# A decoder layer in split float32: weight blocks split in two pieces instead of four, and the pass with the rest of the weights put last

## The chip, the cores and the metric

The kernel runs on one core of a Trainium2 chip. The metric is the device time of one execution, in microseconds (us). An execution uses these engines: TensorE (PE, with its weight loads shown apart as PEld), VectorE (DVE), ScalarE (ACT), GpSimd (POOL), and the DMA queue that SyncE (SP) issues.

## The reference, cut to what matters

One layer of a hybrid decoder on 512 tokens of width 1024, all in float32. An RMS norm; one wide product with w_in, whose columns feed a gated short convolution, a gated delta rule with 8 heads (queries, keys, values, z, and two small gates), and two merge gates; the two branches' output products, merged and projected by w_o; a residual; a second norm; a convolutional FFN of inner width 2816; a final norm.

```python
h = rmsnorm(x, norm_mix_g[l])
proj = h @ w_in[l]
bg, cg, xv, q, k, v, z, a, b, ga, gb = jnp.split(proj, pts, axis=-1)
y_a = short_conv_branch(bg, cg, xv, conv_a_w[l]) @ w_a_out[l]
y_b = gdn_branch(q, k, v, z, a, b, ...) @ w_b_out[l]
mix = jax.nn.sigmoid(ga) * y_a + jax.nn.sigmoid(gb) * y_b
x = x + mix @ w_o[l]
h = rmsnorm(x, norm_ffn_g[l])
x = x + conv_ffn(h, w_up[l], ffn_conv_w[l], w_down[l])
return rmsnorm(x, norm_final_g)
```

## The kernel before

**Three products for one.** Each float32 matrix is split into a rounded part and the rest: w = wh + wl for the weights, x = xh + xl for the activations. A product w x is then three TensorE products, wh xl + wl xh + wh xh, added up in one PSUM bank. The type of the parts is float32r.

**Blocks and jobs.** The weights come in blocks of 1 MB: 8 slices of 128 rows by 256 columns (`col_job`), or 2 slices of 128 rows by all 1024 columns (`row_jobs`, for w_o and w_down). A block is loaded into `raw` by one DMA (L131) and split by `Block.split` (L133 to L146): ACT casts a piece into wh (L143), DVE subtracts it from raw and writes wl (L144). A piece has 512 columns, so a block takes four pieces. raw, wh and wl have two buffers each. `run_jobs` (L148) walks over all blocks in turn: at the head of a job it finishes the split of the job's block, hands the next block's split to the queue `splits`, loads the block after that, and emits the job's products.

**Products.** A column job makes two tiles of 128 output columns by 512 tokens, each in its own PSUM bank, by `products` and `mm3` (L112): with 8 row slices that is 24 products a tile, 48 a block. `mm3` first goes over the 8 slices with a product wh xl and a product wl xh each, and then over the 8 slices with wh xh. A row job has the tokens on the partitions; for each token tile and half of the columns, `part` (L918) makes, for each of its two slices, xl wh, xh wl and xh wh in turn (the activations are the stationary operand there).

**What sets the order.** Every matrix product goes through `mm` (L103). After every fourth product of 512 columns it calls `tick`, which advances the waiting pieces of other work by one step each: the delta rule's scan (`backs`), its triangular inverse (`mids`), its front part (`chains`), two evacuations (`evacs`), and last one piece of the next block's split (`splits`). From this order of emission the framework makes each engine's queue; an engine works its queue in order.

**The start.** x comes as four tiles of 128 tokens. ACT squares and sums a tile (L315), DVE turns the sum into a mean (L320), POOL raises it to the power -1/2 (L321), DVE scales the tile (L326), PE transposes it (L331), and ACT and DVE write the transposed input in its two parts (L341, L343), tiles 0 and 1 as the first half of the tokens, tiles 2 and 3 as the second. The first products (16 gate columns, and the first key block `k_block`) run on the first half while the second is made. For this part the order of DVE, ACT and POOL is that of the program text, written out by hand (L347 on). Around the change it reads:

```python
ks = Task(k_block.split())
norm_x(2)
ks.step()
scale_x(2)
norm_x(3)
ks.step()
scale_x(3)
ks.finish()
```

**The delta rule's stage.** From about 25 to 325 us the products of the four head pairs' queries, keys, values and z run, with the delta rule's small products between them: transposes (L484), the scan (L680 and L681 for the state's reads, whose result DVE completes as r in L683; L693 with r, completed by DVE as vn in L695; L702 and L713 with vn). Then come the short convolution, the merge and w_o, the FFN's first product (two column blocks at a time), and its second.

Of the kernel before, what the change touches and what calls it, by code (L numbers as in the profile page):

```python
# [9 lines left out]
F32 = mybir.dt.float32  # L10
F32R = mybir.dt.float32r
AF = mybir.ActivationFunctionType
ALU = mybir.AluOpType
# [20 lines left out]
class Task:  # L34
    """A stretch of emission that is resumed piece by piece between slabs of matrix products."""

# [21 lines left out]
def layer_kernel(ctx, tc, x, norm_mix_g, w_in, conv_a_w, gdn_conv_w, gdn_A_log, gdn_dt_bias,  # L58
# [20 lines left out]

# [1 line left out]
    chains, mids, backs, evacs, splits = deque(), deque(), deque(), deque(), deque()  # L81
# [17 lines left out]
    def drain(queue):  # L99
        while queue:  # L100
            advance(queue, 1)

    def mm(o, a, b, start, stop):  # L103
        pe.matmul(o, lhsT=a, rhs=b, start=start, stop=stop)  # L104
        nmm[0] += o.shape[-1]
        if nmm[0] >= SLAB * S:
            nmm[0] -= SLAB * S
            tick()
# [3 lines left out]
    def mm3(o, pairs, order=KO):  # L112
        n = len(pairs)
        pairs = [pairs[k] for k in order]
        for i, (ah, al, bh, bl) in enumerate(pairs):
            mm(o, ah, bl, i == 0, False)
            mm(o, al, bh, False, False)
        for i, (ah, al, bh, bl) in enumerate(pairs):
            mm(o, ah, bh, False, i == n - 1)

# [1 line left out]
    class Block:  # L122
# [10 lines left out]
        def split(self):  # L133
            a, b = self.a, self.b
            if self.wh is not None:
                return
            self.wh = wp.tile([P, a, b], F32R, tag="wh", name=nm("wh"))
            self.wl = wp.tile([P, a, b], F32R, tag="wl", name=nm("wl"))
            h = max(1, 512 // b)
            for a0 in range(0, a, h):  # L140
                for b0 in range(0, b, 512):
                    sl = (slice(None), slice(a0, min(a, a0 + h)), slice(b0, min(b, b0 + 512)))
                    act.copy(out=self.wh[sl], in_=self.raw[sl])  # L143
                    dve.tensor_tensor(out=self.wl[sl], in0=self.raw[sl], in1=self.wh[sl].bitcast(F32),  # L144
                                      op=ALU.subtract)
                    yield  # L146

    def run_jobs(jobs):  # L148
        jobs[1][0].load()
        for i, (block, use) in enumerate(jobs):  # L150
            Task(block.split()).finish()
            drain(splits)
            if i + 1 < len(jobs):
                splits.append(Task(jobs[i + 1][0].split()))
            if i + 2 < len(jobs):
                jobs[i + 2][0].load()
            use(block.wh, block.wl)
# [33 lines left out]

# [1 line left out]
    ident = const.tile([P, P], F32, name="ident")  # L193
# [12 lines left out]

# [1 line left out]
    p2 = ExitStack()  # L208
# [6 lines left out]
    tbd = [dram.tile([4, 8, 32, 32], F32, name=f"tbd{p}") for p in range(4)]  # L215
# [1 line left out]
    ab_block = Block(lambda: cols(w_in[0], C_AB, 16), ND, 16)  # L217
    k_block = Block(lambda: cols(w_in[0], C_K, GW), ND, GW)
    HS = S // 2

    # both parts of the 16 columns side by side: two passes give four products
    def ab_products(o, lo, hi):
# [18 lines left out]
    def constants():  # L241
        pool.memset(triu, 1.0)
        pool.affine_select(out=triu, in_=triu, compare_op=ALU.is_ge, fill=0.0, base=0,
                           pattern=[[1, P]], channel_multiplier=-1)
        pool.memset(ones, 1.0)
        # mask16[j, i]: within a block of 32, j in its first half and i in its second
        pool.memset(full, 0.0)
        pool.memset(full.rearrange("p (b t c) -> p b t c", t=2, c=16)[:, :, 1, :], 1.0)
        f3 = full.rearrange("p (b t) -> p b t", t=32)
        pool.affine_select(out=f3, in_=f3, compare_op=ALU.is_ge, fill=0.0, base=0,  # L250
                           pattern=[[-32, 4], [0, 32]], channel_multiplier=1)
        pool.affine_select(out=f3, in_=f3, compare_op=ALU.is_ge, fill=0.0, base=15,
                           pattern=[[32, 4], [0, 32]], channel_multiplier=-1)
        for q in range(4):
            pool.tensor_copy(out=mask16[32 * q:32 * q + 32, :], in_=full[32 * q:32 * q + 32, 32 * q:32 * q + 32])
        # blocks of 16, one to a partition: -1 below the diagonal
        pool.memset(nlow, -1.0)
        pool.affine_select(out=nlow, in_=nlow, compare_op=ALU.is_gt, fill=0.0, base=0,
                           pattern=[[1, 16], [-1, 16]], channel_multiplier=0)
        pool.memset(TTf, 0.0)  # L260
        pool.memset(T64, 0.0)
        for p in range(4):
            nc.sync.dma_start(out=tbd[p].rearrange("q f r c -> (q f r c)").rearrange("(p n) -> p n", p=64),
                              in_=T64.rearrange("p f c -> p (f c)"))

    with tc.tile_pool(name="st1", bufs=1) as st1:
# [80 lines left out]
        with tc.manual_schedule(engines={mybir.EngineType.DVE, mybir.EngineType.Activation, mybir.EngineType.Pool}):  # L347
# [12 lines left out]
            ks = Task(k_block.split())  # L360
# [3 lines left out]
            norm_x(3)  # L364
            ks.step()
            scale_x(3)
# [120 lines left out]
    def front(pr, st):  # L487
# [54 lines left out]
        yield  # L542
        # values and queries by rows
        vs, ssq = tl("vs", 2), tl("ssq", 2, (P, 8))
# [13 lines left out]
        yield VREAD  # L558
        # inverse of the unit triangular factor: blocks of 16 by substitution, then doubled
        dve.tensor_tensor(out=TB, in0=UB.rearrange("p j i -> p i j"), in1=nlow, op=ALU.mult)  # L560
# [101 lines left out]
    def back(pr, st, kn, A, ap_, vs, ssq):  # L662
# [3 lines left out]
        junk = tl("junk", 1, (P, P))  # L666
        # scan over the chunks
        on = vs
# [146 lines left out]

# [1 line left out]
    p3 = ExitStack()  # L817
# [92 lines left out]

# [1 line left out]
    def row_jobs(w, nk, xs, finish, pre, early):  # L912
# [5 lines left out]
        def part(g, t):  # L918
            ts_ = slice(t * P, (t + 1) * P)
            x_ = xs()  # L920
            wh, wl = ws[g]
            for hf in range(2):
                hs = slice(hf * 512, (hf + 1) * 512)
                for kk in range(2):
                    k = 2 * g + kk
                    xh, xl = x_[0][:, k, ts_], x_[1][:, k, ts_]
                    mm(acc[t][hf], xl, wh[:, kk, hs], k == 0, False)
                    mm(acc[t][hf], xh, wl[:, kk, hs], False, False)
                    mm(acc[t][hf], xh, wh[:, kk, hs], False, k == nk - 1)

# [20 lines left out]

# [1 line left out]
    p7 = ExitStack()  # L953
# [49 lines left out]

# [1 line left out]
    gates = {}  # L1005
# [106 lines left out]
```

## Time and profile before

| what | value |
|---|---|
| median of 3 runs | 1000.38 us (999.54 to 1001.76) |
| span of the profiled execution, first to last instruction | 998.5 us |
| median of the runs less that span | 1.9 us |
| PE instructions | 5602 |
| DVE, ACT, POOL instructions | 1090, 931, 101 |
| HBM read and written | 93.27 MB and 3.42 MB, 97 GB/s over the span |
| granted TensorE clock, mean | 0.999 |

The profile lists the profiled execution by its span alone, so the table puts the median of the runs beside it. Busy time is the time in which an engine has at least one instruction under way. TensorE's products overlap, so the length shown for one (0.39 us for 512 columns) is more than the time by which it moves the queue on; that is the distance from one start to the next. A row of a group shows its line, engine, operation, operands and count, then the busy time and the mean length, then the idle time of the engine ahead of it and what ended most of that. A row of the list of waits shows who waited for whom, the total in us, how many times, and the longest. In a timeline a row shows start, length, the instruction and how many were merged into the row.

### The profile page before, as it was taken

To read this page: it belongs to the slowest core of one execution; us is meant where nothing else is said; L and a number is where in the kernel's file an instruction comes from. 1 tells how busy PE (TensorE), PEld (TensorE's weight loads), DVE (VectorE), ACT (ScalarE), POOL (GpSimd) and SP (SyncE) were. 2 spreads that over 40 slices of the span, in tenths; PEclk is the share of its full clock that TensorE was granted. 3 is DMA by queue.
4 is the path that set the end of the run, shared out by engine and by line. 5 is a ranking of instruction groups with operands and counts; after the bars stand their busy time and mean duration, and the time that the engine had idled before them with its cause. 6 is when DMAs were issued, how large, how long until landed. Compare 5 with 4: busy or idle time off the path is not lost.

```text
span 998.5 us, 14009 instructions
## 1 busy us (share of the span) xinstructions
PE 986.6 (99%) x5602; PEld 822.5 (82%) x5602; DVE 545.8 (55%) x1090; ACT 426.2 (43%) x931; POOL 64.3 (6%) x101
## 2 busy tenths in 40 slices
PE   8999999999999999999999999999999999999997
PEld 5887888888888888888888888988888888888886
DVE  6777776897434434542253553675665666532235
ACT  6695666665353322322331232454444444421123
POOL 3331201202010000000000000000000000000000
PEclk9999999999999999999999999999999999999999
DMA  7343232232212232223223252332223223223212
GB/s 223 105 133 94 72 93 86 72 93 57 88 44 85 85 119 93 85 87 124 85 88 124 85 190 84 106 117 96 85 90 121 85 86 126 85 87 124 84 43 85
DMA packets 95409, 97.60 MB, mean 98 GB/s; under 512 B 20299, under 2 KB 88176, under 8 KB 95344
## 3 DMA queue, kind: packets, MB, share of 16 engines
q1 hardware_dynamic: 95344, 96.70, 30.3%
q8 instruction: 44, 0.72, 0.3%
q14 instruction: 21, 0.17, 0.1%
HBM read 93.27 MB, written 3.42 MB: 97 GB/s over the span
## 4 chain that ended last, share of the span: by engine, by line
PE 96%; DVE 1%; issue 1%; ACT 1%; DMA 0%; SPq 0%; POOL 0%; POOLq 0%; ACTq 0%
PE ps L104 88%; PE ps L484 1%; PE ps L519 1%; PE ps L713 1%; PE ps L693 1%; PE ps L702 1%; PE ps L681 1%; PE ps L680 1%; PE ps L656 0%; PE ps L650 0%; DMA raw<-in_w_in_dram 0%; PE ps L991 0%; ACT hT L341 0%; PE ps L603 0%; PE ps L594 0%
## 5 line engine op out<-in xcount | busy, mean ns | idle before, releaser
L104 PE MATMUL ps<-hT,wh 128*128 128x512 f32 (+1 forms) x1184 | 371.2, 391 | 0.3 <-ACT wh L143 0.3
L144 DVE TENSOR_TENSOR wl<-raw,wh 128x512 fp32r<-128x512 f32 x324 | 211.7, 692 | 160.5 <-ACT wh L143 160.1
L104 PEld LDWEIGHTS ps<-hT,wh 128*128 128x128 f32 x1184 | 218.0, 188 | 41.1 <-ACT wh L143 0.6
L143 ACT CAST wh<-raw 128x512 fp32r<-128x512 f32 x324 | 178.6, 618 | 170.5 <-PE ps L104 162.3
L104 PE MATMUL ps<-hT,wl 128*128 128x512 f32 (+1 forms) x592 | 227.0, 385 | 0.3 <-DVE wl L144 0.3
L104 PE MATMUL ps<-h,wh 128*128 128x512 f32 (+1 forms) x768 | 220.8, 372 | 0.0
L104 PEld LDWEIGHTS ps<-h,wh 128*128 128x128 f32 x768 | 140.1, 188 | 24.9
L104 PE MATMUL ps<-h,wl 128*128 128x512 f32 (+1 forms) x384 | 140.2, 371 | 0.0
L104 PEld LDWEIGHTS ps<-hT,wl 128*128 128x128 f32 x592 | 111.4, 188 | 20.5 <-DVE wl L144 0.5
L104 PE MATMUL ps<-wh,aT 128*128 128x512 f32 x352 | 108.5, 389 | 0.0
L104 PEld LDWEIGHTS ps<-h,wl 128*128 128x128 f32 x384 | 72.3, 188 | 12.5
L104 PEld LDWEIGHTS ps<-wh,aT 128*128 128x128 f32 x352 | 66.1, 188 | 13.7
L104 PE MATMUL ps<-wl,aT 128*128 128x512 f32 x176 | 68.5, 389 | 0.0
L188 DVE SCALAR_TENSOR_TENSOR cv<-ps,wA,cv 128x511 f32<-128x511 f32 (+2 forms) x72 | 53.5, 743 | 11.2 <-ACT cv L185 10.4
L188 DVE SCALAR_TENSOR_TENSOR g<-ps,wF,g 128x511 f32<-128x511 f32 (+1 forms) x44 | 32.9, 747 | 48.2 <-ACT g L185 47.9
L188 DVE SCALAR_TENSOR_TENSOR v<-ps,wF,v 128x511 f32<-128x511 f32 (+1 forms) x44 | 32.8, 747 | 34.6 <-ACT v L185 34.3
L104 PE MATMUL ps<-wh,mix 128*128 128x512 f32 x128 | 40.1, 391 | 0.0
L104 PE MATMUL ps<-ya,wh 128*128 128x512 f32 x128 | 39.6, 389 | 0.0
L104 PE MATMUL ps<-yb,wh 128*128 128x512 f32 x128 | 39.6, 389 | 0.0
L104 PEld LDWEIGHTS ps<-wl,aT 128*128 128x128 f32 x176 | 33.0, 188 | 6.9
L185 ACT ACTIVATE g<-ps,wF 128x512 f32<-128x512 f32 x22 | 15.2, 690 | 38.9 <-PE ps L104 38.9
L185 ACT ACTIVATE v<-ps,wF 128x512 f32<-128x512 f32 x22 | 15.2, 690 | 38.6 <-PE ps L104 38.6
(227 smaller groups left out, 970.0 us busy)
## 6 DMA issues: line engine op xcount, KB each, us to landing
raw<-in_w_in_dram SPq DMA_DIRECT2D x36, 1024.0 KB, 5.1
raw<-in_w_up_dram SPq DMA_DIRECT2D x22, 1024.0 KB, 5.1
raw<-in_w_down_dram SPq DMA_DIRECT2D x11, 1024.0 KB, 4.9
raw<-in_w_a_out_dram SPq DMA_DIRECT2D x4, 1024.0 KB, 5.7
raw<-in_w_b_out_dram SPq DMA_DIRECT2D x4, 1024.0 KB, 5.6
raw<-in_w_o_dram SPq DMA_DIRECT2D x4, 1024.0 KB, 6.7
Dm<-gtd SPq DMA_DIRECT2D x4, 512.0 KB, 3.9
x<-in_x_dram SPq DMA_DIRECT2D x4, 512.0 KB, 6.8
```

The source lines that it names most:

```text
L104: pe.matmul(o, lhsT=a, rhs=b, start=start, stop=stop)
L143: act.copy(out=self.wh[sl], in_=self.raw[sl])
L144: dve.tensor_tensor(out=self.wl[sl], in0=self.raw[sl], in1=self.wh[sl].bitcast(F32), op=ALU.subtract)
L185: act.activation(out=dst, in_=src, func=AF.Copy, scale=wcol(taps - 1))
L188: dve.scalar_tensor_tensor(out=dst[:, sh:], in0=src[:, :S - sh], scalar=wcol(j), in1=dst[:, sh:], op0=ALU.mult, op1=ALU.add)
L484: pe.transpose(out=o[:, n * P:(n + 1) * P], in_=src[:, n * P:(n + 1) * P], identity=ident)
L519: pe.matmul(o[:, i], lhsT=kqs[:, a, h, 0, sl], rhs=kqs[:, b, h, :, sl], start=a > 0, stop=a + b == 0)
L680: pe.matmul(o[:, 0:P], lhsT=kq[:, h, 0, sl], rhs=St[h], start=True, stop=True)
L681: pe.matmul(o[:, P:2 * P], lhsT=kq[:, h, 1, sl], rhs=St[h], start=True, stop=True)
L693: pe.matmul(o[:, 0:P], lhsT=TTf[:, f, :], rhs=rs[h], start=True, stop=True)
L702: pe.matmul(o2[:, 0:P], lhsT=kn[:, f, :], rhs=vns[h], start=True, stop=True)
L713: pe.matmul(o[:, 0:P], lhsT=A[:, f, :], rhs=vns[h], start=True, stop=True)
```

## The change

Four edits that belong to the two in the title; the rest of the diff takes out comments and moves nothing.

- `mm3`: three loops over the slices instead of two: wh xh, then wh xl, then wl xh. The pass with the rest of the weights comes last.
- `part` in the row jobs: for both slices xh wh and xl wh, then for both slices xh wl.
- `Block.split`: a step takes half of the block's slices with all their columns, 4 x 256 or 1 x 1024, which is 1024 columns. A block takes two steps instead of four. In the start one `ks.step()` is taken out, so the key block's two steps are the first `ks.step()` and `ks.finish()`.
- `run_jobs`: `drain(splits)` stands ahead of finishing the job's own split instead of behind it.

```diff
         for i, (ah, al, bh, bl) in enumerate(pairs):
-            mm(o, ah, bl, i == 0, False)
-            mm(o, al, bh, False, False)
+            mm(o, ah, bh, i == 0, False)
+        for ah, al, bh, bl in pairs:
+            mm(o, ah, bl, False, False)
         for i, (ah, al, bh, bl) in enumerate(pairs):
-            mm(o, ah, bh, False, i == n - 1)
+            mm(o, al, bh, False, i == n - 1)
...
-            h = max(1, 512 // b)
-            for a0 in range(0, a, h):
-                for b0 in range(0, b, 512):
-                    sl = (slice(None), slice(a0, min(a, a0 + h)), slice(b0, min(b, b0 + 512)))
-                    act.copy(out=self.wh[sl], in_=self.raw[sl])
-                    dve.tensor_tensor(out=self.wl[sl], in0=self.raw[sl], in1=self.wh[sl].bitcast(F32),
-                                      op=ALU.subtract)
-                    yield
+            for a0 in range(0, a, a // 2):
+                sl = (slice(None), slice(a0, a0 + a // 2))
+                act.copy(out=self.wh[sl], in_=self.raw[sl])
+                dve.tensor_tensor(out=self.wl[sl], in0=self.raw[sl], in1=self.wh[sl].bitcast(F32),
+                                  op=ALU.subtract)
+                yield
...
         for i, (block, use) in enumerate(jobs):
+            drain(splits)
             Task(block.split()).finish()
-            drain(splits)
...
             norm_x(3)
-            ks.step()
             scale_x(3)
             ks.finish()
...
-                for kk in range(2):
-                    k = 2 * g + kk
-                    xh, xl = x_[0][:, k, ts_], x_[1][:, k, ts_]
-                    mm(acc[t][hf], xl, wh[:, kk, hs], k == 0, False)
-                    mm(acc[t][hf], xh, wl[:, kk, hs], False, False)
-                    mm(acc[t][hf], xh, wh[:, kk, hs], False, k == nk - 1)
+                xs_ = [(kk, x_[0][:, 2 * g + kk, ts_], x_[1][:, 2 * g + kk, ts_]) for kk in range(2)]
+                for kk, xh, xl in xs_:
+                    mm(acc[t][hf], xh, wh[:, kk, hs], 2 * g + kk == 0, False)
+                    mm(acc[t][hf], xl, wh[:, kk, hs], False, False)
+                for kk, xh, xl in xs_:
+                    mm(acc[t][hf], xh, wl[:, kk, hs], False, 2 * g + kk == nk - 1)
```

## The prediction

> **What bounds the kernel now.** I read the profile page first, then the busy times by stretch, then the list of TensorE's (PE's) own waits, and last the timelines of the places that these point to.
>
> ```profile
> span 998.5 us, 14009 instructions
> PE 986.6 (99%) x5602; PEld 822.5 (82%) x5602; DVE 545.8 (55%) x1090; ACT 426.2 (43%) x931; POOL 64.3 (6%) x101
> ...
> 0.00:25.00 25.00, 20.29 (x119) 14.59 (x120) 16.51 (x40) 17.12 (x39) 8.95 (x27) 1.00 0.73 223
> 25.00:325.00 300.00, 299.26 (x2438) 251.69 (x2436) 206.28 (x540) 176.98 (x473) 50.65 (x66) 1.00 0.29 85
> 325.00:992.00 667.00, 667.00 (x3050) 556.22 (x3048) 320.90 (x507) 230.47 (x417) 4.12 (x7) 1.00 0.30 99
> 992.00:998.50 6.50, 0.02 (x1) 0.00 (x0) 2.12 (x6) 1.59 (x5) 0.54 (x1) 0.78 0.21 81
> ```
>
> The rows by stretch give its length, then the busy time of PE, weight load, DVE (VectorE), ACT (ScalarE) and POOL, then the granted clock. From 325 to 992 us PE has no idle time at all, from 25 to 325 us it lacks 0.74 us, in the first 25 us it lacks 4.7 us, and the last 6.5 us are the end after its last product. DVE and ACT are well below full in every stretch. So the kernel is a queue of matrix products, and time can come or go in three ways only: idle PE at the start, idle PE in the gated-delta-rule stage (25 to 325 us), or another pace of the products.
>
> ```profile
> PE ps L484 <- DVE vs L732: 0.7, 1, 0.7
> PE ps L331 <- DVE xr L326: 0.6, 1, 0.6
> PE ps L104 <- DVE wl L144: 0.3, 1, 0.3
> PE ps L104 <- ACT wh L143: 0.3, 1, 0.3
> ```
>
> These are PE's waits, apart from two before 8 us. The split of the weights (wh on L143, the rest wl on L144) holds PE up twice, 0.3 us each, both in the first block. Nowhere later does PE wait for weights.
>
> The pace of the products is read from two timelines, one of the FFN's first product and one of its second (start, length, instructions merged into the line):
>
> ```profile
> 755.89 0.39 PE L104 MATMUL ps<-h,wl 128*128 128x512 f32 x1
> 756.12 2.20 PE L104 MATMUL ps<-h,wh 128*128 128x512 f32 x9
> 758.16 0.39 PE L104 MATMUL ps<-h,wl 128*128 128x512 f32 x1
> ...
> 905.04 0.39 PE L104 MATMUL ps<-wl,aT 128*128 128x512 f32 x1
> 905.27 0.61 PE L104 MATMUL ps<-wh,aT 128*128 128x512 f32 x2
> 905.72 0.39 PE L104 MATMUL ps<-wl,aT 128*128 128x512 f32 x1
> ```
>
> A run of nine wh products advances by (758.16 - 756.12) / 9 = 0.227 us each. A wl product followed by a wh product advances by 0.23. In the second FFN product three take 0.68 us, again 0.227 each. Runs and alternation cost the same.
>
> **The change, part by part.** *Order of the passes.* The number of products, their shapes and their count per PSUM bank stay as they are. At 0.227 us in a run and in alternation the new order costs nothing, as long as pace depends only on shape. It also keeps the place of the other engines' work: that is handed out after every fourth product, whichever pass it belongs to. What moves is which half of a block is needed when. wl is wanted 16 products (3.6 us) into each tile instead of at its first product, and wh is released eight products (1.8 us) before the end of a block instead of at the end, wl the other way round. PE never waits for either after the start, so I cost this at nothing. The cover is the whole block: 48 products of 0.227 us are 10.9 us, in which two new pieces, one behind the other on two engines, take about 3.5. Were the cover gone, each block would wait a first cast and a first subtract, about 2.3 us.
>
> *Swap of the two statements at the head of a job.* Where a split has been started, both orders finish it before the products; where it hasn't, both emit all of it there. Nothing changes.
>
> *Pieces of 1024 columns.* 324 casts and 324 subtracts become 162 of each. The rows for the price of a piece:
>
> ```profile
> L144 DVE TENSOR_TENSOR wl<-raw,wh 128x512 fp32r<-128x512 f32 x324 | 211.7, 692 | 160.5 <-ACT wh L143 160.1
> L231 DVE TENSOR_TENSOR ab<-raw,ab 128x128 fp32r<-128x128 f32 x1 | 0.3, 286 | 0.0
> L143 ACT CAST wh<-raw 128x512 fp32r<-128x512 f32 x324 | 178.6, 618 | 170.5 <-PE ps L104 162.3
> L230 ACT CAST ab<-raw 128x128 fp32r<-128x128 f32 x1 | 0.3, 300 | 0.2 <-DMA raw<-in_w_in_dram 0.2
> ```
>
> DVE: (692 - 286) / 384 = 1.06 ns a column, so 692 + 512 x 1.06 = 1.23 us. ACT: (618 - 300) / 384 = 0.83 ns, so 618 + 424 = 1.04 us. Busy time falls to 162 x 1.23 = 199 us on DVE (from 211.7) and 162 x 1.04 = 169 us on ACT (from 178.6): some 12 and 10 us, on engines that don't set the end. After the start that is worth nothing.
>
> *The start.* Here a longer piece matters, because ACT, DVE and POOL work in an order written out by hand. It runs: norm of x tile 2, piece of k, scale of tile 2, norm of tile 3, piece of k, scale of tile 3, rest of k. The change takes the second "piece of k" out and makes the first one twice as long.
>
> ```profile
> 14.02 0.67 ACT L143 CAST wh<-raw 128x512 fp32r<-128x512 f32 x1
> ...
> 14.71 0.69 DVE L144 TENSOR_TENSOR wl<-raw,wh 128x512 fp32r<-128x512 f32 x1 [0.35 <-ACT wh L143]
> ...
> 14.73 0.38 PE L104 MATMUL ps<-hT,wh 128*128 128x256 f32 x1 [0.30 <-ACT wh L143]
> 15.32 0.75 DVE L326 TENSOR_SCALAR xr<-xt,rt 128x1024 f32<-128x1024 f32 x1
> ...
> 15.46 0.38 PE L104 MATMUL ps<-hT,wl 128*128 128x256 f32 x1 [0.35 <-DVE wl L144]
> ...
> 15.69 0.28 PE L104 MATMUL ps<-hT,wh 128*128 128x256 f32 x1
> ...
> 15.80 0.28 PE L104 MATMUL ps<-hT,wl 128*128 128x256 f32 x1
> 15.98 0.15 DVE L320 TENSOR_SCALAR rt<-sst 128x1 f32<-128x1 f32 x1
> 16.21 0.55 POOL L321 TENSOR_TENSOR rt<-rt,nhalf 128x1 f32<-128x1 f32 x1 [1.22 <-DVE rt L320]
> 16.22 0.41 PE L331 MATMUL ps<-ident,xr 128*128 128x128 f32 x2
> ...
> 16.88 0.75 DVE L326 TENSOR_SCALAR xr<-xt,rt 128x1024 f32<-128x1024 f32 x1
> ```
>
> Before: the cast ends at 14.69, the subtract runs from 14.71, the scale of tile 2 (L326) starts at 15.32 and ends at 16.07, and PE transposes from 16.22. Ahead of that PE has done four products of k (14.73 to 15.80). After: the cast runs 14.02 to 15.06, the subtract from 15.10 to 16.33. DVE starts an instruction some 0.08 us before the last one's end (15.32 against 14.71 + 0.69), so the scale starts at 16.25, ends at 17.00, and PE can transpose from 17.15. The longer piece holds half of the k slices instead of a quarter, and the new order needs only wh first, so PE again has four products of that tile to do (from 15.1 to 15.6) and then nothing that stands ahead of the transposes. At 17.15 it is where it was at 16.22: 0.93 us late.
>
> Does this heal later? Queued behind the longer subtract on DVE are that scale, then the mean of tile 3 (15.98 before, now 16.9), POOL's power behind it, then the scale of tile 3: 17.8 instead of 16.88. Those feed the second half of the transposed input, so it is late by the same amount and the distances stay. From 17.15 PE has work without a gap: eight transposes, then 12 products that need only wh (its second cast ends near 17.1), then the transposes of tile 3, then the wl pass. With PE full from there to 992 us nothing gives the time back.
>
> The bounds: a piece of 0.75 us, the DVE row for 1024 columns of another operation, would make it +0.45, and so would four products of the second k tile, if they come forward into the gap (4 x 0.12). Two old pieces behind each other, 2 x 0.69 = 1.38, would make it +1.08. I take 0.93, because the 512 and 128 column rows are the same operation. [...]
>
> *The sum.* 998.5 us of span + 0.93 = 999.4. The median of the three runs is 1000.38, 1.9 us above the profiled span, which I carry over: **1001.3 us**.
>
> **The rivals.** *Stalls in the delta-rule scan (slower).* Between 25 and 325 us DVE is 69% busy, and the scan goes PE, DVE, PE. A longer subtract in front of a scan step makes PE's queue wait. One such place, DVE's rows and then PE's next step:
>
> ```profile
> 297.93 1.29 DVE L144 TENSOR_TENSOR wl<-raw,wh 128x512 fp32r<-128x512 f32 x2
> 299.13 0.60 DVE L683 SCALAR_TENSOR_TENSOR r<-ps,neG,vs 128x128 f32<-128x128 f32 x2
> 299.65 0.68 DVE L144 TENSOR_TENSOR wl<-raw,wh 128x512 fp32r<-128x512 f32 x1
> 300.51 0.61 DVE L695 TENSOR_SCALAR vn<-ps,ap 128x128 f32<-128x128 f32 x2 [0.17 <-PE ps L693]
> ...
> 301.46 0.61 PE L702 MATMUL ps<-vn,kn 128*128 128x128 f32 x4
> ...
> L144 DVE TENSOR_TENSOR wl<-raw,wh 128x512 fp32r<-128x512 f32 x78 | 53.5, 711 | 10.9 <-ACT wh L143 10.7
> ```
>
> With 1.23 us the piece at 299.65 would end at 300.88, and vn would start at 300.80 instead of 300.51: 0.29 late, against 301.46 - 301.12 = 0.34 us of slack before PE's step. That speaks against, and so does the row at 297.93: two old pieces back to back already take 1.29 us ahead of a scan step. For it speaks that 0.05 us is thin and that one wait of 0.7 us on DVE stands there today. The stage holds 78 / 2 = 39 new pieces; if eight cost the full 0.29, that is 2.3 us on top of the start: 1003.6. It decides from four such pieces on (four are 1.2 us, which takes the sum over 1002.4). [...]
>
> *The gap closes instead (faster).* The first wl wait (0.35) goes because wl comes last, the start's loss is filled by other products, and less DVE time lets the 0.74 us wait in the delta-rule stage go: 1000.38 - 0.35 - 0.74 = 999.3. The wait at L484 follows a POOL operation rather than a split, which speaks against. [...] If the start's loss alone is filled, the time stays at 1000.4.
>
> *The order changes the pace.* The new order puts products with the same moving operand, or the same kind of stationary one, behind each other in ways that the trace doesn't show. One ns on each of the 3050 TensorE instructions between 325 and 992 us is 3.05 us: 1004.4, or 998.2 the other way. The equal 0.227 us in run and alternation speaks against both.
>
> **How the numbers follow.** Forecast 1001.3 (own range 1000.6 to 1002.2): 0.56. Scan stalls, 1003.6: 0.18. Gap closed or nothing moved, 999.3 to 1000.4: 0.18. Another pace: 0.08, half each way. A measurement of this kernel can tell about 0.2% from no change, which is 998.4 to 1002.4. Slower: 0.15 of the scan's 0.18, 0.04 of the pace and 0.05 of the forecast's upper edge, 0.24. Faster: 0.04 of the pace and 0.02 of the closed gap, 0.06. Within: 0.70. The range 999.0 to 1003.8 leaves out the pace (0.08) and about 0.11 at the ends of the scan stalls and of the closed gap.
>
> **What would show it.** Right: 162 casts near 1.04 us and 162 subtracts near 1.23; tile 2's transposes from about 17.1 us; PE full from 325 us to its last product at 0.227 us each; no new waits of PE over 0.3 us between 25 and 325 us. Wrong: the transposes at 16.3 or earlier, products between the four first ones and the transposes, a list of scan steps (L693, L702, L713, L680) among PE's waits, or a pace other than 0.227.

## The result, and the profile after

The changed kernel takes 1014.63 us (median of 4 runs, 1012.75 to 1015.88), beside 1000.01 us of the kernel before on the same chip (4 runs, 999.54 to 1001.76). The ratio is 1.0141, 95% interval 1.0124 to 1.0157: the change costs 14.6 us where 0.9 were forecast. The profiled execution took 1015.88 us. Its page, and its busy times by the same stretches as above (length, then PE, weight load, DVE, ACT, POOL, granted clock):

```profile
span 1014.1 us, 13727 instructions
PE 994.9 (98%) x5602; PEld 827.1 (82%) x5602; DVE 534.1 (53%) x928; ACT 412.1 (41%) x769; POOL 62.4 (6%) x101
```

```profile
0.00:25.00 25.00, 19.74 (x100) 13.97 (x101) 15.33 (x34) 16.57 (x35) 9.93 (x27) 0.93 0.70 219
25.00:325.00 300.00, 292.47 (x2384) 243.91 (x2383) 197.54 (x492) 168.04 (x429) 47.38 (x67) 0.98 0.29 82
325.00:992.00 667.00, 667.00 (x3055) 556.52 (x3054) 309.62 (x379) 219.49 (x288) 2.96 (x5) 1.00 0.30 98
```

From 325 us on nothing has changed: PE is full, with 3055 instructions in 667 us against 3050 before. In the delta-rule stage it now lacks 7.5 us where it lacked 0.74, and the clock, which stood at 1.00, is at 0.98. The list of PE's waits names the places:

```profile
PE ps L592 <- DMA T<-tbd: 3.9, 3, 3.6
PE ps L601 <- DVE TT L585: 2.0, 1, 2.0
...
PE ps L104 <- ACT wh L142: 1.4, 1, 1.4
PE ps L330 <- DVE rt L319: 1.3, 1, 1.3
...
PE ps L700 <- DVE vn L693: 0.3, 1, 0.3
```

(The changed kernel's lines stand one or two below those of before: L592 is L594 there, L601 is L603, L700 is L702, L142 and L143 are L143 and L144.) The third and fourth lie in the first 25 us. The first two are new. They belong to the inverse of head pair 0, which the prediction doesn't name. DVE solves 16 x 16 blocks by substitution, 14 steps of two small instructions, into TB. Two DMAs write TB to DRAM (tbd), four more read it back in another layout as T. PE then makes two sets of 64 small products, the first with T (L592), the second with the first one's result and TT, DVE's transpose of T (L601). PE's timeline at that place, before and after:

```profile
90.68 0.75 PE L594 MATMUL ps<-T,um 32*32 32x32 f32 x64
91.36 2.11 PE L104 MATMUL ps<-hT,wh 128*128 128x512 f32 x8
93.41 0.75 PE L603 MATMUL ps<-Y,TT 32*32 32x32 f32 x64
```

```profile
92.88 1.98 PE L104 MATMUL ps<-hT,wl 128*128 128x512 f32 x8
98.43 0.22 PE L592 MATMUL ps<-T,um 32*32 32x32 f32 x2 [3.58 <-DMA T<-tbd]
98.82 0.69 PE L592 MATMUL ps<-T,um 32*32 32x32 f32 x4 [0.17 <-DMA T<-tbd]
99.67 1.03 PE L592 MATMUL ps<-T,um 32*32 32x32 f32 x58 [0.16 <-DMA T<-tbd]
102.73 1.08 PE L601 MATMUL ps<-Y,TT 32*32 32x32 f32 x64 [2.03 <-DVE TT L585]
103.74 3.80 PE L104 MATMUL ps<-hT,wh 128*128 128x512 f32 x8
...
113.31 0.66 PE L482 MATMUL ps<-ident,kq 128*128 128x128 f32 x4
```

Before, PE finds T ready and runs eight products between the two sets. After, it stands 3.6 us for T and 2.0 us for TT, with nothing between the sets. Behind that, eight products take 3.80 us where eight took 2.11. The stretches say why:

```profile
94.00:98.50 4.50, 0.92 (x6) 0.47 (x4) 3.56 (x4) 2.70 (x5) 0.00 (x0) 1.00 0.47 98
98.50:104.00 5.50, 3.02 (x129) 2.56 (x130) 2.75 (x6) 1.52 (x3) 0.00 (x0) 0.53 0.67 203
104.00:112.50 8.50, 8.50 (x62) 5.91 (x64) 0.73 (x2) 1.53 (x4) 1.57 (x4) 0.50 0.01 2
```

The granted clock falls to half: 5.5 x (1 - 0.53) x 2 = 5.2 us of the second stretch and all 8.5 of the third, 13.7 us in all. In the 4.5 us of the first stretch, just ahead of the fall, PE had 0.92 us of work.

T is late because the substitution is. Its rows before and after, from the queries on its tile (count, duration min/median/max, first and last start):

```profile
L566 DVE TENSOR_TENSOR sub<-UB,TB x14: 147/196/208, 69.5 to 76.4; 64x14 f32<-64x14 f32 x2, 64x26 f32<-64x26 f32 x2, 64x36 f32<-64x36 f32 x2, 64x44 f32<-64x44 f32 x2
```

```profile
L564 DVE TENSOR_TENSOR sub<-UB,TB x14: 144/188/207, 77.0 to 91.7; 64x14 f32<-64x14 f32 x2, 64x26 f32<-64x26 f32 x2, 64x36 f32<-64x36 f32 x2, 64x44 f32<-64x44 f32 x2
```

It starts 7.5 us later, and it takes 14.7 us from first to last step instead of 6.9. The steps are no longer; from the ninth on, DVE's queue has other rows between them, convolution taps of 0.7 us and pieces of 1.2, one of which waits 1.9 us for ACT. The later start comes from ACT's queue: the squares of the keys, whose last one kn (the scaled keys) waits for, start at 54.04 us instead of 49.63, behind two more table loads of 1.28 us, and have a 1.05 us cast, the 2.45 us of exponentials (Dm) and another table load among them. kn's second half is late by 9.4 us:

```profile
53.31 0.68 DVE L505 TENSOR_TENSOR kn<-ps,kdv 128x512 f32<-128x512 f32 x1
```

```profile
62.75 0.69 DVE L503 TENSOR_TENSOR kn<-ps,kdv 128x512 f32<-128x512 f32 x1 [1.33 <-ACT junk L502]
```

T's reading by the four DMAs, before and after (first and last start, and the time from a start to the landing of its data):

```profile
L579 SPq DMA_DIRECT2D T<-tbd x4: 303/448/664, 79.6 to 81.2; - x4
...
DMA to landing us min/median/max: 3.5/3.6/3.8
```

```profile
L577 SPq DMA_DIRECT2D T<-tbd x4: 303/448/451, 96.4 to 97.8; - x4
...
DMA to landing us min/median/max: 1.8/1.8/1.9
```

So T was complete at about 84.6 us before, 6.0 us ahead of PE at 90.68. Now it is complete at about 99.5, 4.7 us after PE is done with the last product in front of it (92.88 + 1.98 = 94.86), and the last 58 small products start at 99.67. From the start of TB's writing to the start of T's reading it takes 3.8 us instead of 2.3 (92.63 to 96.43, 77.31 to 79.63), but the reading itself lands 1.8 us faster, so T is late by what the substitution is late.

**Where the 15.6 us between the spans lie.** For every PE instruction I took the distance to the next start less a nominal time, taken from these traces (0.227 us for 512 columns, 0.120 for 256, 0.110 for 128, 0.059 and 0.010 for the small ones), and summed what is left, in us, by stretch:

| kernel | span | 0-25 | 25-80 | 80-125 | 125-326 | half clock in 0-25 and in 80-125 |
|---|---|---|---|---|---|---|
| before | 998.5 | 9.0 | 0.8 | 2.6 | 9.8 | 0, 0 |
| after | 1014.1 | 11.3 | 0.8 | 13.6 | 12.2 | 3.4, 13.7 |

Start 2.3, pair 0's inverse 11.0, the rest of the stage 2.3. After 326 us the sums of these two agree to 0.1.

### The profile page after: what moved, and what is told of

Read it like the earlier page. It is cut to its first block, busy times and chain, and to the rows that moved or that the text cites. A ratio compares the mean times of both kernels' runs of the same rounds, so it can differ in the third digit from the quotient of the medians.

```text
span 1014.1 us, 13727 instructions
## 1 busy us (share of the span) xinstructions
PE 994.9 (98%) x5602; PEld 827.1 (82%) x5602; DVE 534.1 (53%) x928; ACT 412.1 (41%) x769; POOL 62.4 (6%) x101
## 4 chain that ended last, share of the span: by engine, by line
PE 95%; DVE 2%; issue 1%; ACT 1%; DMA 1%; SPq 0%; POOL 0%; POOLq 0%; DVEq 0%; ACTq 0%
PE ps L104 86%; PE ps L482 1%; PE ps L517 1%; DMA xt<-in_x_dram 1%; DVE wl L143 1%; PE ps L711 1%; PE ps L700 1%; PE ps L691 1%; PE ps L679 0%; PE ps L678 0%; PE ps L654 0%; PE ps L648 0%; DVE cv L187 0%; PE ps L989 0%; PE ps L601 0%
## 5 line engine op out<-in xcount | busy, mean ns | idle before, releaser
L143 DVE TENSOR_TENSOR wl<-raw,wh 128x1024 fp32r<-128x1024 f32 x162 | 198.0, 1239 | 221.0 <-ACT wh L142 157.7
L104 PE MATMUL ps<-hT,wh 128*128 128x512 f32 (+1 forms) x1184 | 292.6, 393 | 1.4 <-ACT wh L142 1.4
L142 ACT CAST wh<-raw 128x1024 fp32r<-128x1024 f32 x162 | 163.2, 1049 | 216.1 <-PE ps L104 205.1
L104 PE MATMUL ps<-h,wh 128*128 128x512 f32 (+1 forms) x768 | 168.8, 372 | 0.0
L104 PE MATMUL ps<-hT,wl 128*128 128x512 f32 (+1 forms) x592 | 148.9, 390 | 0.0
L104 PE MATMUL ps<-wh,aT 128*128 128x512 f32 x352 | 94.1, 389 | 0.0
L104 PE MATMUL ps<-h,wl 128*128 128x512 f32 (+1 forms) x384 | 88.1, 371 | 0.0
L104 PE MATMUL ps<-wl,aT 128*128 128x512 f32 x176 | 54.2, 389 | 0.0
L187 DVE SCALAR_TENSOR_TENSOR g<-ps,wF,g 128x511 f32<-128x511 f32 (+1 forms) x44 | 32.8, 747 | 10.7 <-ACT g L184 10.3
L180 ACT CAST aT<-v 128x512 fp32r<-128x512 f32 x22 | 13.7, 621 | 60.7 <-DVE v L1029 60.7
L1019 ACT ACTIVATE g<-g 128x512 f32<-128x512 f32 x22 | 13.9, 632 | 47.1 <-DVE g L187 47.1
```

The lines of the kernel that those rows point to most:

```text
L180: act.copy(out=dst[0][:, idx], in_=src)
L187: dve.scalar_tensor_tensor(out=dst[:, sh:], in0=src[:, :S - sh], scalar=wcol(j), in1=dst[:, sh:], op0=ALU.mult, op1=ALU.add)
L1019: act.activation(out=t, in_=t, func=AF.Silu)
```

## The experiments

First three theories. **A**: the new order of the passes alone reorders the queues. **B**: the longer pieces do it. **C**: the later start pushes all else past its place. Then one account, from the runs: PE's place for the inverse is fixed in its queue, and T misses it. All ratios are to the kernel before, run on the same chip.

**1. The new order alone.** The kernel before with the new `mm3` and `part`, pieces of 512 columns and the old start.

> The kernel before with the new order of the passes alone (pieces of 512 columns, start as before). Theory A, queue order: the new order changes when a tile's evacuation can begin and with it the order in which ScalarE and VectorE take the steps of the first head pair's inverse, so TensorE waits for the inverse here too: a wait of over 2 us between 85 and 125 us, and 1006 to 1012 us. Theory B, piece length: no such wait, and 999 to 1001 us, since 0.227 us a product holds in any order. Theory C, late start: as B, 999 to 1001 us.

Measured: 1011.1 us, ratio 1.0113 (1.0084 to 1.0141).

**2. The longer pieces alone.** The kernel before with the new `Block.split` and without the second `ks.step()` in the start.

> The kernel before with pieces of 1024 columns alone (old order of the passes; the start with two steps of the key block instead of four). Theory A, queue order by the passes: only the start is later, 1000.5 to 1002.5 us, and no wait over 1 us between 85 and 125 us. Theory B, piece length: the wait for the inverse's data of 3.6 us is there, 1009 to 1014 us. Theory C, late start: the start is late here too, so the wait is there as well, 1009 to 1014 us.

Measured: 1013.25 us, ratio 1.0122 (1.0099 to 1.0144).

Each edit alone costs nearly as much as both, so the costs don't add up and neither edit has a price of its own. Run 1 is what A expected and run 2 what B and C did, so none of the three is the whole cause. The wait for T is there in both (first row the order, second the pieces):

```profile
PE ps L596 <- DMA T<-tbd: 4.3, 4, 3.4
```

```profile
PE ps L591 <- DMA T<-tbd: 5.1, 4, 4.2
```

And so is the spread of the substitution:

```profile
L568 DVE TENSOR_TENSOR sub<-UB,TB x14: 145/188/211, 74.1 to 86.8; 64x14 f32<-64x14 f32 x2, 64x26 f32<-64x26 f32 x2, 64x36 f32<-64x36 f32 x2, 64x44 f32<-64x44 f32 x2
```

```profile
L563 DVE TENSOR_TENSOR sub<-UB,TB x14: 147/190/211, 77.8 to 89.6; 64x14 f32<-64x14 f32 x2, 64x26 f32<-64x26 f32 x2, 64x36 f32<-64x36 f32 x2, 64x44 f32<-64x44 f32 x2
```

Ahead of it they go different ways: with the order alone kn's second half comes at 58.9 us, with the pieces alone at 54.5 (53.3 before). Two different shuffles of the queues end in the same place.

**3. The start with four pieces.** The changed kernel, the key block alone in four pieces at the four old places.

```diff
-k_block = Block(lambda: cols(w_in[0], C_K, GW), ND, GW)
+k_block = Block(lambda: cols(w_in[0], C_K, GW), ND, GW, 4)   # pieces
...
             norm_x(3)
+            ks.step()
             scale_x(3)
```

> The changed kernel with the key block, and it alone, split in four pieces of 512 columns at the old places of the start. Theory C, late start: the start is back, the first pair's steps come in time, the wait goes and the time is 1000 to 1003 us. Theories A and B: the start gives back 1 to 2.3 us, the wait of some 5.6 us for the inverse and the half clock after it stay: 1011.5 to 1013.5 us.

Measured: 1013.05 us, ratio 1.0123 (1.0101 to 1.0144); the wait for T is still there, 4.3 us. Theory C falls, though not by this run alone: the new order of the key block's products stayed, and this profile lost 12.0 us in its first 25, so the start itself didn't come back. Run 1 is the stronger case: it lost 8.6 us there, no more than the kernel before, and has the wait all the same.

**4. A later place, for all pairs.** The changed kernel with `Y_T`, the number of steps that the inverse is held back, at 24 instead of 17.

> The changed kernel with the inverse's products put 24 instead of 17 ticks after its front part (28 products of 0.227 us, 6.4 us later in TensorE's queue). All three theories put about 11 of the 14.6 us down to TensorE's queue standing at those products with data on the way, 5.6 us of wait and the rest a half clock after it. If so, the wait goes, the clock stays at 1.00 between 85 and 125 us, and the time is 1002.5 to 1005 us. If the inverse is late by more than its place (a later scan then waits instead), 1008 us or more.

Measured: 1010.46 us, ratio 1.0103 (1.0079 to 1.0126). The wait for T is gone, and another has come, at 203 us, with 3.4 us of half clock behind it:

```profile
PE ps L482 <- DVE vs L730: 4.3, 2, 3.7
```

**5. The substitution kept together.** The changed kernel; pair 0's 28 instructions are emitted at once, and what DVE is given in the next 80 steps is queued behind the last of them (`r`).

```diff
+            if j == 14 and pr == 0:
+                Task.tc, Task.hold, Task.left = tc, r.ins, 80
...
-            if j % 3 == 0:
+            if j % 3 == 0 and pr:
                 yield
...
+            if Task.left:
+                Task.left -= 1
+                with Task.tc.issue_after(Task.hold):
+                    got = next(self.gen, self)
```

> The changed kernel, but in pair 0 the 28 steps of the substitution stand directly behind each other in DVE's queue, and what DVE is given in the next 80 emission steps stands behind them; PE's queue keeps the inverse at the same place. In the changed kernel those steps are spread over 15.6 us among other rows, in the kernel before they take 7.8. If the loss is the inverse standing too early in PE's queue for a T that comes late: the substitution starts at about 75 us and takes 7.8, T is read near 88 us, PE gets to its step near 94, so neither the 3.6 us wait nor the half clock behind it is there: about 11 us less than the changed kernel, 1003 to 1005 us, with the 2.3 us of the start and some small waits left. If the loss comes from the new order or the longer pieces as such (PE held up by weights, slower products), it stays at 1013 to 1015. If the work pushed behind the substitution is missed instead, new waits of PE on cv or wl at 84 to 92 us: 1006 to 1010.

Measured: 1007.11 us, ratio 1.0059 (1.0046 to 1.0072): 8.2 us of the 14.1 (by the ratios, of 1000) are back. The substitution starts as late as in the changed kernel and takes 5.9 us:

```profile
L571 DVE TENSOR_TENSOR sub<-UB,TB x14: 147/195/209, 76.5 to 82.4; 64x14 f32<-64x14 f32 x2, 64x26 f32<-64x26 f32 x2, 64x36 f32<-64x36 f32 x2, 64x44 f32<-64x44 f32 x2
```

The wait for T and the half clock behind it are gone. I had expected 1003 to 1005; what I missed is that PE still has no product between the two sets and now waits for the first one's result: `Y`, 1.4 us.

**6. Extra products in the first idle time.** The changed kernel with 14 products of 0.227 us more, placed eight products ahead of the first set.

```diff
+        for _ in range(14 if pr == 0 else 0):
+            pe.matmul(o, lhsT=hT[0][:, 0, 0:P], rhs=hT[0][:, 0, :], start=True, stop=True)
```

> The changed kernel with 14 more products (128x128 by 128x512, 0.227 us each, 3.2 us in all, into the bank of the inverse's first step, which overwrites them) ahead of the last eight products before the inverse of pair 0. T comes as late as before (98.4 us), so the extra work lies inside the 3.6 us wait and what is left of that is some 0.4 us. If the clock falls because PE was idle, it now stays full: the 13.65 us at half clock go, which cost 6.8: 1007.8 us. If the halved clock has another cause (the small products, or a power limit), nothing is won: 1014.6, or 1017.8 if the extra products move T too.

Measured: 1014.2 us, ratio 1.0128 (1.0115 to 1.0142); not the 1007.8 that I expected. T came 0.8 us later, 1.9 us of the first wait were left, the second (2.3 us) stayed, and with it half of the half clock: 6.8 us instead of 13.7.

**7. Substitution together, and the start as before.** Run 5, and besides four pieces and the old order of passes for the key block.

> The substitution kept together as in the first run of this call, and the start as before the change as well: the key block in four pieces of 512 columns at the four old places, and its two tiles in the old order of passes. If the start is the other 2.3 us of the loss and nothing else of the change costs time: 1000 to 1002 us, level with the kernel before. If the pass order or the longer pieces cost something in the rest of the delta-rule stage: 1003 or more. A gain below 999 is expected by neither.

Measured: 1006.0 us, ratio 1.0047 (1.0034 to 1.0060), worse than expected: the same 1.4 us wait for Y was followed here by 3.4 us of half clock.

**8. The change from job 20 on.** The kernel before; order and pieces switch when the delta-rule stage is over, for 120 of the 162 new steps.

```diff
     def open_conv():
+        old[0] = False
```

> The kernel before, with the change (order of passes and pieces of 1024 columns) switched on only when the delta-rule stage is over, from about 312 us on, some two thirds of all blocks. If the change costs only by what it does to the queues of the delta-rule stage: 1000.2 us, within 0.5 of the kernel before, PE full from 325 us to its last product. If order or piece length cost something everywhere (pace, weights late): about two thirds of the loss, 1009 us.

Measured: 1000.96 us against 1001.06, ratio 1.0000 (0.9991 to 1.0009). Order and pieces cost nothing behind the delta-rule stage, where PE is full:

```profile
325.00:992.00 667.00, 667.00 (x3051) 556.87 (x3050) 312.45 (x385) 222.00 (x297) 3.81 (x7) 1.00 0.30 98
```

**9. Together, start as before, and a later place for pair 0.** Run 7 with

```diff
-        for _ in range(Y_T):
+        for _ in range(Y_T if pr else 22):
```

> The kernel of the run that kept the substitution together and restored the start (1006.0 us), and besides the inverse of pair 0, and of no other pair, is put 5 steps later in the emission (22 instead of 17), which puts 8 products between its first and its second small product where there were none. That kernel lost its last 4 us between 80 and 125 us: 1.4 us in which PE waits for Y, the result of the first small product on its way through ACT, and 3.4 us of half clock behind it. If place against readiness is the whole cause, both go: 1001 to 1003 us, what is left being 1 to 2 us of small waits of the scan. If moving the inverse only hands the wait on, as in the run that moved it for all pairs, a wait of 3 to 4 us comes in later and it stays at 1005 or more.

Measured: 1004.02 us, ratio 1.0031 (1.0021 to 1.0042), a little above the band. Between 80 and 125 us all is as before the change (2.6 us in the table below), with products between the sets again:

```profile
94.98 0.75 PE L614 MATMUL ps<-T,um 32*32 32x32 f32 x64
...
97.06 1.17 PE L111 MATMUL ps<-hT,wl 128*128 128x512 f32 x4
98.16 0.75 PE L623 MATMUL ps<-Y,TT 32*32 32x32 f32 x64
```

What is left lies in the scan, 12.2 us against 9.8.

**10. One number.** The changed kernel with pair 0's place alone at 24.

> The changed kernel with one number changed: the inverse of pair 0 alone is put 7 steps later (24 instead of 17); substitution, start, order and pieces stay as in the changed kernel. T then comes at 96 to 98 us, before PE gets to it. If the loss is that one place: the waits on T and the half clock at 99 us go, and the later pairs keep their places, so 1002 to 1005 us. If the later start of pair 0's scan is handed on to pair 1, as with 24 for all pairs (1010.5 us): a wait of about 4 us near 200 us and 1009 to 1011.

Measured: 1005.06 us, ratio 1.0047 (1.0033 to 1.0061). 9.4 us of the 14.1 (by the ratios, of 1000) come back with everything else of the change in place. Between 80 and 330 us PE waits 0.2 us for vn, and otherwise only:

```profile
PE ps L482 <- DVE vs L730: 1.4, 2, 0.7
```

**11. The control.** The kernel before with pair 0's place at 22.

> Control: the kernel before with the inverse of pair 0 put 5 steps later (22 instead of 17), and nothing else. Before the change T is ready some 6 us ahead of its place, so a later place wins nothing; if the scan of pair 0 has slack behind it, it costs nothing either: 1000.2 us, within 0.7. If a later place is better by itself, whatever the change did, it comes out below 999; if pair 0's scan has no slack, at 1002 or more.

Measured: 1002.33 us, ratio 1.0016 (1.0006 to 1.0027). A later place is not better by itself; the scan behind it pays 1.9 us (11.7 against 9.8 in the last stretch). The 2.4 us that run 9 had left in the same stretch are of this size; how much of them is the later place was not measured apart.

**12. Both idle times filled.** The changed kernel with 16 products ahead of the first set and 9 between the two, written into banks that the sets overwrite.

> The changed kernel with both idle times at pair 0's inverse filled with extra products of 0.227 us: 16 (3.6 us) ahead of the last eight products before the first small product, and 9 (2.0 us) between the first and the second small product; they go into banks that the small products overwrite. T stays late, so the small products stand where they stood or up to 0.9 us later, as in the run with 14. There the first idle time was nearly filled, the second not, and half of the 13.65 us of half clock stayed. If the half clock comes from idle time of PE and from nothing else, it is gone here: the changed kernel less 6.8 us, plus up to 0.9: 1007.8 to 1008.7 us, and no half clock between 95 and 125 us. If the many small products or something else call it up, 3.4 us or more of it stays and the time is 1011 to 1014.

Measured: 1012.12 us, ratio 1.0107 (1.0090 to 1.0124). The clock stays full through the place where it was at 0.53 and 0.50:

```profile
98.50:104.00 5.50, 4.11 (x77) 3.01 (x76) 4.36 (x6) 1.06 (x2) 0.00 (x0) 1.00 0.20 29
104.00:112.50 8.50, 8.50 (x172) 6.59 (x171) 1.76 (x4) 4.52 (x13) 1.57 (x4) 1.00 0.38 124
```

The small products are all still there, and of the waits of 3.9 and 2.0 us are left 1.4, for T, in four parts: at this place the half clock went with the idle time, and the small products alone didn't call it up. (Run 12 lost 1.1 us more than the changed kernel in its first 25, with 6.8 us of half clock there instead of 3.4.) The price that I had put on it, 13.65 / 2 = 6.8 us, is too high, since part of those 13.7 us is waiting anyway. The same work, from the first product after the second set to the next transposes, takes 113.31 - 103.74 = 9.6 us in the changed kernel and here, by the two rows below, 110.97 - 105.23 = 5.7: 3.8 us, plus a little for the slower small products.

```profile
105.23 2.14 PE L104 MATMUL ps<-hT,wh 128*128 128x512 f32 x8
...
110.97 0.66 PE L482 MATMUL ps<-ident,kq 128*128 128x128 f32 x4
```

The same sums as above for all runs, by span:

| kernel | span | 0-25 | 25-80 | 80-125 | 125-326 | half clock |
|---|---|---|---|---|---|---|
| 8, from job 20 | 1000.0 | 10.4 | 0.7 | 2.6 | 9.9 | 3.4, 0 |
| 9, together, start, place | 1000.6 | 8.6 | 0.9 | 2.6 | 12.2 | 0, 0 |
| 11, before, place | 1000.8 | 9.5 | 0.7 | 2.6 | 11.7 | 3.4, 0 |
| 10, after, place of pair 0 | 1003.4 | 9.9 | 0.9 | 3.7 | 12.7 | 0, 0 |
| 7, together, start | 1003.9 | 8.9 | 0.9 | 6.8 | 11.0 | 0, 3.4 |
| 5, together | 1004.9 | 11.0 | 0.8 | 5.2 | 11.8 | 3.4, 0 |
| 1, order | 1007.3 | 8.6 | 0.7 | 10.7 | 11.0 | 0, 6.8 |
| 4, all places | 1008.6 | 11.0 | 0.7 | 3.7 | 16.9 | 3.4, 0 |
| 12, both filled | 1010.7 | 12.4 | 0.7 | 4.5 and 5.7 of extra products | 11.1 | 6.8, 0 |
| 2, pieces | 1012.0 | 10.0 | 0.7 | 13.7 | 10.2 | 0, 13.7 |
| 3, four pieces at the start | 1012.3 | 12.0 | 0.8 | 11.2 | 12.0 | 6.8, 6.8 |
| 6, first filled | 1013.0 | 11.4 | 0.8 | 9.3 and 3.2 of extra products | 12.2 | 3.4, 6.8 |

Run 2's row sums to 12.4 us more than that of before and its span is 13.5 longer; the rest lies behind 326 us, 0.8 of it in one wait for the second norm (hn). No version beats the kernel before.

## Why the prediction was wrong

**The step that failed** is in the part on the order of the passes: "It also keeps the place of the other engines' work". The place in the emission is kept; the place in the queues is not. ACT's and DVE's queues came out in another order with either edit alone (runs 1 and 2), and so did PE's, which lost the eight products between the two sets. What was costed at nothing made PE wait 4.3 and 5.1 us for T in these runs and cost 11 and 12 us. The second half of the same error is the sentence on the pieces: 12 and 10 us less work "on engines that don't set the end" is worth nothing. DVE and ACT did set the end here, where PE's queue held steps for them (waits of 3.9 and 2.0 us), and busy shares of 69% and less don't show that. The profile of before gave the margin: T is complete at 84.6 us, PE comes to it at 90.68, and a substitution that comes later or takes longer eats those 6.0 us. I looked for thin places in PE's waits and DVE's scan steps, where the last instruction is late, and not at a chain through DVE, a write and a read by DMA, and PE, whose place in the queue is fixed.

**The sum lacked a term for the clock.** The wait of 3.6 us and the one of 2.0 behind it were paid again in the products that followed, by 3.8 us (9.6 in the changed kernel, 5.7 in run 12). Of the 11.0 us at the inverse about 5.9 are waits (3.9 and 2.0) and about 4 the clock; the rest I can't assign. The start pays such a term too, as its own paragraph below shows.

**Right.** The pieces: 1.23 and 1.04 us were worked out. A group's row shows count, then busy time and mean in ns:

```profile
L143 DVE TENSOR_TENSOR wl<-raw,wh 128x1024 fp32r<-128x1024 f32 x162 | 198.0, 1239 | 221.0 <-ACT wh L142 157.7
L142 ACT CAST wh<-raw 128x1024 fp32r<-128x1024 f32 x162 | 163.2, 1049 | 216.1 <-PE ps L104 205.1
```

The pace: 0.227 us a product in any order, by the full stretch from 325 us and by run 8. That rival falls, and so does "the gap closes".

**The start: the size about right, the clock again left out.** Forecast +0.93; the changed kernel lost 2.3 more in its first 25 us. Of that, some 1.3 us is the half clock: it stood from 16.88 to 20.29 us, and 12 products of 256 columns advance there by 0.226 us each instead of 0.120:

```profile
16.90 0.44 PE L330 MATMUL ps<-ident,xr 128*128 128x128 f32 x1 [1.28 <-DVE rt L319]
...
17.00 2.91 PE L104 MATMUL ps<-hT,wh 128*128 128x256 f32 x12
...
19.71 0.91 PE L104 MATMUL ps<-hT,wl 128*128 128x256 f32 x4
```

The kernels sorted by the half clock in their first 25 us say the same. With none, the old start lost 8.8 us in the mean (before, 7, 9) and the new one 9.9 (10); with 3.4 us, the old one 10.0 (8, 11) and the new one 11.2 (after, 4, 5, 6): +1.1 and +1.2, rough figures, since 8 and 11, with the same start, differ by 0.9. Run 2, with the longer pieces alone and no half clock, lost 10.0, run 1, with the order alone and none, 8.6. Why some executions have the half clock there and others not stays open. The transposes of tile 2 began at 16.90, 0.68 us later than before and not the 0.93 that was worked out, and only one of the 16 transposes of the second half came there; 14 came from 21.05 on. So PE's queue had another order than the prediction took for granted here too.

**The scan rival: right in place and size, not shown in its cause, and not the main loss.** It was priced at 2.3 us in the delta-rule stage, from a longer subtract that makes DVE's vn late for L702. The last stretch did lose 2.3, and nearly all of it lies ahead of that very step: the distances in front of it hold 0.05 us above nominal before, 2.4 after, 1.0 with the order alone and 0.2 with the pieces alone. That speaks against the longer subtract as the cause by itself, and the agreement of 2.3 with 2.3 is luck as far as the runs show. The rows on vn of the changed kernel show part of it, where before PE isn't in the list of those who waited:

```profile
who waited for it (us, times):
...
  PEld ps L700: 1.0, 2
...
  PE ps L700: 0.3, 1
```

**The length of the pieces doesn't decide alone.** Run 2 loses 12 us with the long pieces, but run 1 loses 11 with pieces of unchanged length, and run 10 wins two thirds of the 14.1 back with the long ones.

**Open.** Why the framework's queues come out as they do was not tried; that it reckons T as late and therefore moves PE's products ahead of the first set is only argued. Nor was it tried whether a shorter DVE piece alone removes the 2.3 us of the scan.

## What to carry to other kernels

Where one engine is full and the others feed it at fixed places of its queue, price a change by the margin of each feeding chain, the time from "ready" to the place where the full engine needs it, and not by the feeders' busy time. An edit that moves emission or instruction length can reorder queues that it never names, so compare the order of every engine around the thinnest margin. A late feeder can be cured at its place: one number won back 9 of 14 us here, but the chain behind pays for a place that is too late (run 11: 1.9 us).

## What the runs showed of the hardware

In the stretches of the tables the half clock lasted 3.4, 6.8 or 13.7 us, where there was any. In the changed kernel's trace the clock changes at 16.88, 20.29, 98.80, 112.45 and 1010.15 us; the distances from one to the next, 3.41, 78.51, 13.65 and 897.70 us, are 1, 23, 4 and 263 times 3.413. The wait just ahead of a fall was not equally long each time: 3.58 us ahead of 98.80 in the changed kernel, 1.35 in run 7. Runs 5 and 7 have the same instructions in the same order around the inverse and the same wait:

```profile
97.72 0.75 PE L614 MATMUL ps<-Y,TT 32*32 32x32 f32 x64 [1.35 <-ACT Y L607]
98.40 2.56 PE L111 MATMUL ps<-hT,wh 128*128 128x512 f32 x10
```

```profile
95.76 0.75 PE L623 MATMUL ps<-Y,TT 32*32 32x32 f32 x64 [1.35 <-ACT Y L616]
96.45 4.16 PE L111 MATMUL ps<-hT,wh 128*128 128x512 f32 x10
```

In run 7 ten products behind it took 4.16 us, at half clock, in run 5 they took 2.56. The first row below is run 7's 3.41 us ahead of the fall at 96.55, the second a stretch of run 5 that is about as long and holds its wait:

```profile
93.14:96.55 3.41, 2.06 (x127) 1.61 (x126) 2.64 (x4) 2.70 (x5) 0.00 (x0) 1.00 0.26 82
```

```profile
95.99:99.41 3.42, 2.07 (x111) 1.77 (x98) 2.41 (x3) 2.83 (x5) 0.00 (x0) 1.00 0.06 14
```

PE was busy equally long in both stretches, 2.06 and 2.07 us, but products of 512 columns had 0.54 us of that in run 7 and 1.01 in run 5 (from 98.40 on), the small ones the rest. In the 3.41 us ahead of run 6's fall, 98.53 to 101.94, PE stood for 2.07 us and had small products alone. So neither the length of the wait nor PE's busy time in these two rows tells runs 5 and 7 apart, and why one fell and the other didn't was not shown.
